# Weight operands made ahead and parked in DRAM, one unsplit intermediate, and last projections without GpSimd in a two-block kernel

## The chip, the cores and the metric

The kernel runs on one core of a Trainium2 chip. The metric is device time in microseconds for one launch. The time before is 2069.35 us, the median of three runs from 2067.27 to 2070.33. The profile shown is one execution by itself.

## The reference

Two blocks run one after the other on a sequence of 1024 tokens of width 1024, in fp32. The first has a mixer (three-pattern attention, a diagonal state-space branch, two gates) and a gated feed-forward part with a causal convolution. The second has three gated branches, whose projections are summed. Cut to what matters here:

```python
def _conv_ffn(u, w_up, w_conv, b_conv, w_down):        # block one
    a, val = jnp.split(u @ w_up, 2, axis=-1)           # 1024 -> 2 x 2048
    conv = b_conv
    for j in range(CONV_W):
        conv = conv + w_conv[j] * shifted(a, j)
    return (jax.nn.silu(conv) * val) @ w_down          # f, 2048 -> 1024

def _hybrid_layer(x, ...):                             # block two
    h = _rmsnorm_2(x, norm_g)
    p = h @ w_in                                       # 1024 -> 7680, twelve pieces
    ...
    y_a = (gmlp(u, v) * silu(z_a)) @ w_pa              # 512 -> 1024, three times
    y_b = (shortconv(x_b, b_g, c_g) * silu(z_b)) @ w_pb
    y_c = (pool(x_c) * silu(z_c)) @ w_pc
    merged = sigmoid(g_a) * y_a + sigmoid(g_b) * y_b + sigmoid(g_c) * y_c
    return x + merged @ w_o
```

## The kernel before

**Arithmetic.** Each fp32 operand of a product is split in two parts of type fp32r, high and low: ScalarE casts it (high), VectorE or GpSimd subtracts (low); `split` does both. Each product then takes three matmuls. A matmul here has 128 rows by 128 columns of weights and 512 moving columns.

**Strassen pairs.** The products with `w_up` (stage `ffn`) and with `w_in_2` (stages `gb` to `uz`) are made by seven products of half size rather than eight. The activations are combined into operands `s1` to `s4`, `a22` and others (class `X` in the code, four pieces k each, so that X.s2.3 is the piece 3 of s2); two blocks of weights make one pair, and are combined into b11, b21, t1 to t4 and b22 (class `Weights`). The weight sums are GpSimd operations (`pool` in `make`), the splits are ScalarE casts and VectorE subtractions. I write (0, t4) for the operand t4 of pair 0.

**Pairs begun early.** The activations come in two halves of tokens or rows, and the first half is ready sooner. For the first `NPF` = 4 pairs of `ffn` and the first `NPRE` = 6 of `gb` and `v2`, the products that need only the early half are made first, while `w_out` or the end of `down` (`lastdown`) still runs, with b11 and b21. Their other five operands, t2, t3, t1, t4 and b22, are made by the `late` entries of `make`, when the stage itself starts.

**Order.** The kernel first writes down all operations (class `Plan`); a list scheduler in it then orders them for all engines, by its own estimates, with limits on the buffers of each group (`nc.glim`). Each engine's queue runs in that order. That is why every instruction of the profile has line 458 (`issue`). `LEADR`, `LEADD`, `FLEAD` are the numbers of operations by which a load may be put ahead.

**Weights.** `Stream` walks a list of weight items (`_ITEMS`): `dma_to` loads ahead on SP's queue, `split_to` splits ahead, `get` gives a split item, `take` a raw one. `st.sa` says how many items ahead are split; it is 0 in the last stages.

**Stages**, by the trace, in us: v, us, gates and qk to 325; attn to 540; y1 to 605; w_out to 696; ffn to 1031; down to 1199; lastdown to 1258; gb to 1314; v2, B, C, gc, ga, uz to 1814; spat to 1834; yb to 1883; yc to 1926; ya to 1970; wo to the end.

**f.** `ffn` makes f in 16 tiles of 128 features by 1024 tokens, splits it and writes both parts to DRAM (`fs_d`), 32 writes on GpSimd's queue. `down` loads both parts again on SP's queue, half of the tokens at a time (`th` = 0, 1; 64 loads of 256 KB), multiplies each with the split weights `w_down` in steps `c` of two feature tiles, 48 matmuls for four row tiles, and, after the first half, transposes the rows for block two (`u3_tr`).

**Last projections.** `yb`, `yc` and `ya` run `gated`: for each item of weights the projection, times its gate, added to `mt`. The input of the next projection (`spilled`) is loaded and split; for `yc`, whose input is `cc_d`, the subtraction is GpSimd's, during `yb`. The additions to `mt` are GpSimd's in yb and yc.

Of the kernel before, what the change touches and what calls it, by code (L numbers as in the profile page):

```python
# [59 lines left out]
LEADR = 120  # L60
# [28 lines left out]
def _items():  # L89
# [384 lines left out]
def kernel(ctx: ExitStack, tc: tile.TileContext, x, wts, wada, vecs, rows, ssmv, wglu, ttab, iden,  # L474
# [11 lines left out]
    nc.glim = {"r": 5, "w": 14, "rr": NRR, "w2": NW2, "o": NO}  # L486
# [49 lines left out]
    fs_d = [dtile(f"f{i}_d", 16, F32R) for i in range(2)]  # L536
# [62 lines left out]
    class Stream:  # L599
# [159 lines left out]
    class Weights:  # L759


        def __init__(self, nk, order):
# [11 lines left out]
        def make(self, order):  # L774
            h = self.h

            def pool(o, a, b, op):
                nc.gpsimd.tensor_tensor(out=o, in0=a, in1=b, op=op)

            raws = {}  # L780
            for what, key in order:
# [3 lines left out]
                if what in ("pair", "early0", "late"):  # L785
# [8 lines left out]
                if what != "late":  # L794
                    self.operand((key, "b11"), b11)
                    yield
                    if what == "early0":
                        continue
# [21 lines left out]
        def pop(self, key):  # L820
# [1122 lines left out]
    for t in proj_half(me, 1, xsrc, hB, rowt):  # L1943
        if t % 4 == 0:
# [19 lines left out]
    W = Weights(4, early(NPF) + [("late", i) for i in range(NPF)] + [("pair", i) for i in range(NPF, 16)])  # L1964
# [12 lines left out]
    for i, n in enumerate(UPS):  # L1977
# [51 lines left out]
    for k in range(DAHEAD):  # L2029
        load_f(k, 0)  # L2030
    for th in range(2):
        full = [mm_ps(), mm_ps()]
        a, b = full
        pt = [[a[:, 0:512], a[:, 512:1024]], [b[:, 0:512], b[:, 512:1024]]] + [[tr_ps(), tr_ps()] for _ in range(2)]
        for c in range(7):
            w = [wA1(st.get()) for _ in range(2)]
# [19 lines left out]
        for i in range(2):  # L2056
            n = 16 * th + 14 + i + DAHEAD
            if n < 32:
                load_f(n % 16, n // 16)
# [393 lines left out]
```

## Time and profile before

| what | us |
|---|---|
| median of three runs | 2069.35 |
| the profiled execution, its own time | 2067.5 |
| its span in the trace | 2065.8 |
| TensorE busy | 1980.1 (96%) |
| VectorE busy | 1419.0 (69%) |
| ScalarE busy | 814.5 (39%) |
| GpSimd busy | 574.9 (28%) |

The mean granted TensorE clock is 0.982 of full speed. The trace gives each engine's instructions with start and length. An engine's idle time is put down to what released the instruction after it. The chain is followed back from the last instruction, always to what came last. Because TensorE is busy for nearly all of the span, a stretch is best read by counting its matmuls against its length.

### The profile page before, as it was taken

To read this page: it belongs to the slowest core of one execution; us is meant where nothing else is said; L and a number is where in the kernel's file an instruction comes from. 1 tells how busy PE (TensorE), PEld (TensorE's weight loads), DVE (VectorE), ACT (ScalarE), POOL (GpSimd) and SP (SyncE) were. 2 spreads that over 40 slices of the span, in tenths; PEclk is the share of its full clock that TensorE was granted. 3 is DMA by queue.
4 is the path that set the end of the run, shared out by engine and by line. 5 is a ranking of instruction groups with operands and counts; after the bars stand their busy time and mean duration, and the time that the engine had idled before them with its cause. 6 is when DMAs were issued, how large, how long until landed. Compare 5 with 4: busy or idle time off the path is not lost.

```text
span 2065.8 us, 24834 instructions
## 1 busy us (share of the span) xinstructions
PE 1980.1 (96%) x9174; PEld 1632.9 (79%) x9174; DVE 1419.0 (69%) x2246; ACT 814.5 (39%) x1277; POOL 574.9 (28%) x523
## 2 busy tenths in 40 slices
PE   5999999999999979999999998999999999989998
PEld 3788888888888757888888876887888888867887
DVE  8767765787664799777744469678878654673645
ACT  4413334667321634434432444343433433451212
POOL 4200202223201374333202038324323433121320
PEclk7999999999999999999999999999999999999999
DMA  8345444331833313423595513413212332264312
GB/s 338 113 156 194 165 146 107 102 100 57 319 129 142 118 51 131 145 92 119 194 355 174 209 71 134 152 45 109 86 70 95 128 112 105 71 244 143 112 52 82
DMA packets 88809, 282.23 MB, mean 137 GB/s; under 512 B 10224, under 2 KB 14672, under 8 KB 88688
## 3 DMA queue, kind: packets, MB, share of 16 engines
q1 hardware_dynamic: 58896, 186.72, 25.8%
q0 software_dynamic: 29792, 93.93, 13.3%
q8 instruction: 72, 1.18, 0.2%
q14 instruction: 49, 0.40, 0.1%
HBM read 206.62 MB, written 65.01 MB: 131 GB/s over the span
## 4 chain that ended last, share of the span: by engine, by line
PE 80%; issue 7%; DVE 6%; POOL 3%; DMA 2%; ACT 1%; SPq 0%; POOLq 0%; ACTq 0%; DVEq 0%
PE mm L458 41%; PE tr L458 39%; DVE s L458 6%; POOL s L458 3%; ACT s L458 1%; DMA s<-s 1%; DMA gs_d<-s 0%; DVE sm L458 0%; DMA s<-in_x_dram 0%; DMA vq_d<-s 0%; DMA g_d<-s 0%; DMA s<-in_wts_dram 0%; DMA v_d<-s 0%; SPq L458 0%; POOL gs_d L458 0%
## 5 line engine op out<-in xcount | busy, mean ns | idle before, releaser
L458 PE MATMUL mm<-s,s 128*128 128x512 f32 (+1 forms) x4424 | 1056.7, 394 | 28.8 <-DVE s L458 24.9
L458 PEld LDWEIGHTS mm<-s,s 128*128 128x128 f32 x4424 | 834.0, 190 | 209.8 <-DVE s L458 32.1
L458 PE MATMUL tr<-s,s 128*128 128x512 f32 (+3 forms) x4080 | 917.6, 378 | 25.1 <-DVE s L458 9.1
L458 PEld LDWEIGHTS tr<-s,s 128*128 128x128 f32 (+1 forms) x4080 | 719.6, 188 | 169.4 <-ACT s L458 15.6
L458 DVE TENSOR_TENSOR s<-s,s 128x512 fp32r<-128x512 f32 (+11 forms) x699 | 669.3, 986 | 149.2 <-ACT s L458 108.5
L458 ACT CAST s<-s 128x512 fp32r<-128x512 f32 (+4 forms) x556 | 382.7, 719 | 490.2 <-PE mm L458 161.0
L458 POOL TENSOR_TENSOR s<-s,s 128x512 f32<-128x512 f32 (+5 forms) x183 | 290.1, 1592 | 585.0 <-ACT s L458 317.4
L458 ACT ACTIVATE s<-s 128x1024 f32<-128x1024 f32 (+3 forms) x151 | 143.4, 952 | 318.5 <-DVE s L458 292.0
L458 DVE TENSOR_TENSOR s<-s,mm 128x512 f32<-128x512 f32 x184 | 125.5, 683 | 121.4 <-PE mm L458 120.8
L458 POOL TENSOR_TENSOR s<-s 128x512 f32<-128x512 f32 x92 | 141.9, 1545 | 118.1 <-DMA s<-in_wts_dram 58.9
L458 ACT COPY s<-tr 128x512 f32<-128x512 f32 (+2 forms) x160 | 85.0, 537 | 145.3 <-PE tr L458 143.0
L458 DVE SCALAR_TENSOR_TENSOR s<-s,s 128x1024 f32<-128x1024 f32 (+1 forms) x65 | 84.8, 1311 | 45.6 <-ACT s L458 44.3
L458 ACT ACTIVATE s<-s,sm 128x512 f32<-128x512 f32 (+7 forms) x119 | 90.6, 774 | 51.2 <-DVE sm L458 50.6
L458 DVE TENSOR_TENSOR s<-tr,s 128x512 fp32r<-128x512 f32 (+3 forms) x105 | 66.8, 652 | 61.6 <-PE tr L458 42.9
L458 PE MATMUL tr<-idn,s 128*128 128x128 f32 x608 | 92.8, 279 | 13.2 <-ACT s L458 8.5
L458 PEld LDWEIGHTS tr<-idn,s 128*128 128x128 f32 x608 | 74.0, 144 | 32.1 <-ACT s L458 11.9
L458 DVE SCALAR_TENSOR_TENSOR s<-s,mm 128x1024 f32<-128x1024 f32 x40 | 48.7, 1219 | 58.1 <-PE mm L458 58.1
L458 DVE TENSOR_TENSOR s<-s,tr 128x512 f32<-128x512 f32 (+1 forms) x90 | 52.6, 587 | 10.8 <-PE tr L458 5.2
L458 DVE SCALAR_TENSOR_TENSOR s<-s,vt,s 128x1023 f32<-128x1023 f32 (+1 forms) x40 | 54.7, 1368 | 4.4 <-ACT s L458 4.1
L458 POOL DMA_DIRECT2D f_d<-s x32 | 17.5, 548 | 114.1 <-ACT s L458 101.0
L458 ACT ACTIVATE s<-mm,hb 128x1024 f32<-128x1024 f32 x15 | 16.8, 1117 | 75.5 <-PE mm L458 67.0
L458 POOL DMA_DIRECT2D s<-s x48 | 25.2, 534 | 75.6 <-ACT s L458 60.8
(103 smaller groups left out, 654.6 us busy)
## 6 DMA issues: line engine op xcount, KB each, us to landing
s<-in_wts_dram SPq DMA_DIRECT2D x193, 512.0 KB, 4.3
s<-in_wada_dram SPq DMA_DIRECT2D x48, 512.0 KB, 5.9
f_d<-s POOLq DMA_DIRECT2D x32, 512.0 KB, 3.2
s<-f_d SPq DMA_DIRECT2D x64, 256.0 KB, 6.4
g_d<-s POOLq DMA_DIRECT2D x24, 512.0 KB, 3.1
s<-g_d SPq DMA_DIRECT2D x24, 512.0 KB, 8.4
s<-s POOLq DMA_DIRECT2D x32, 256.0 KB, 4.6
s<-in_x_dram SPq DMA_DIRECT2D x8, 512.0 KB, 9.0
```

The costliest lines, as they stand in the source:

```text
L458: hook(getattr(getattr(self.nc, eng), method)(*args, **kw), self.ops[i][7] + f"|{self.start[i]:.0f}|{i}")
```

## The change

It has five parts.

1. **Late operands.** A new generator, `store`, makes the five late operands of a pair ahead of their stage: it loads the pair's two raw blocks (SP's queue), makes the four sums on VectorE, splits (ScalarE and VectorE) and writes each operand, 512 KB, to DRAM (`wd_d`, GpSimd's queue). The 4 pairs of `ffn` are stored during `y1` and `w_out`, one step for each tile; the 6 of `gb` and `v2` during `down`, three or four steps for each `c`. Where `make` had `late` entries, it has `stored` ones: five loads on SP's queue, up to `LEADS` = 150 operations ahead. The raw blocks for this are appended to the items.
2. **f unsplit.** `ffn` writes f as it is, 16 writes. `down` loads it and splits it there (`load_f`, `split_f`).
3. **down's second half** makes the first three steps for row tiles 0 and 1, then `u3_tr`, and only then those steps for row tiles 2 and 3.
4. **Last projections.** The split of `cc_d` and the additions to `mt` go from GpSimd to VectorE, and from `spat` on `st.sa` is 2.
5. `LEADR` goes from 120 to 140.

Operations in the program: VectorE from 2182 to 2250, ScalarE from 1155 to 1171, GpSimd from 519 to 501, SP from 409 to 427, TensorE 9062 in both.

```diff
+SA2 = 2
+LATE = ("t2", "t3", "t1", "t4", "b22")
+LEADS = 150
-LEADR = 120
+LEADR = 140
...
+            def fetch(key, name):
+                t = slot("wb", F32R, group="w2")
+                load(f32(t), f32(wd_d[self.base + key][name]), nc.sync, LEADS)
+                self.w[key, name] = t[:, 0:h], t[:, 512:512 + h]
...
+                if what == "stored":
+                    for name in LATE:
+                        fetch(key, name)
+                        yield
...
+    def store(keys):
+        for key in keys:
+            r = [slot("r", group="ps") for _ in range(2)]
+            for i in range(2):
+                load(r[i], wts[_NITEM + 2 * key + i], nc.sync, LEADS)
+            (b11, b21), (b12, b22) = ((t[:, 0:512], t[:, 512:1024]) for t in r)
+            def put(name, src):
+                t = slot("ws", F32R, group="ps")
+                split(t[:, 0:512], t[:, 512:1024], src)
+                nc.gpsimd.dma_start(out=wd_d[key][name], in_=t)
+            tt(b12, b22, b12, ALU.subtract)
+            tt(b11, b12, b11, ALU.add)
+            yield
+            put("t2", b11)
...
-        hi, lo = slot("fh", F32R), slot("fl", F32R)
-        split(hi, lo, pv)
-        nc.gpsimd.dma_start(out=fs_d[0][n], in_=hi)
-        nc.gpsimd.dma_start(out=fs_d[1][n], in_=lo)
+        nc.gpsimd.dma_start(out=f_d[n], in_=pv)
...
+    def split_f(m):
+        if m < 16:
+            r = fr.pop(m)
+            for i in range(2):
+                t = ft[2 * (m % 8) + i, m // 8] = slot("f", F32R)
+                split(t[:, 0:512], t[:, 512:1024], r[:, 512 * i:512 * i + 512])
...
+    st.sa = SA2
...
-            split(hi, lo, f, None, e)
+            split(hi, lo, f)
...
-                (tt if last else lambda o, x_, y_, op: nc.gpsimd.tensor_tensor(out=o, in0=x_, in1=y_, op=op))(
-                    g, g, mt[n + j], ALU.add)
+                tt(g, g, mt[n + j], ALU.add)
```

In the rows of the order, a name such as s_7004 is one tile in SBUF, tr_ and mm_ are PSUM; the number counts tiles in the order of the plan. VectorE at ffn's start, before: the first row is X.s2.0, `s_6959` and `s_6952` are the raw blocks of pair 0, `s_7009`, `s_7090` and `s_7147` the sums behind X.s2.1 to X.s2.3.

```order
L458 TENSOR_TENSOR s_7004<-s_6981,s_7004 128x512
L458 TENSOR_TENSOR s_7022<-s_6959,s_7022 128x512
L458 TENSOR_TENSOR s_7009<-s_7009,s_6748 128x512
L458 TENSOR_TENSOR s_7017<-s_6952,s_7017 128x512
L458 TENSOR_TENSOR s_7069<-s_7009,s_7069 128x512
L458 TENSOR_TENSOR s_7090<-s_6993 128x512
L458 TENSOR_TENSOR s_7063<-s_6959,s_7063 128x512
L458 TENSOR_TENSOR s_7097<-s_6952,s_7097 128x512
L458 TENSOR_TENSOR s_7090<-s_7090,s_6788 128x512
L458 TENSOR_TENSOR s_6986<-s_6952,s_6986 128x512
L458 TENSOR_TENSOR s_7128<-s_7090,s_7128 128x512
L458 TENSOR_TENSOR s_7147<-s_7011 128x512
```

The five rows that read `s_6959` or `s_6952` are (0, t2), (0, t3), (0, t4), (0, t1) and (0, b22); X.s2.3 comes five rows behind the last one shown. The same place of VectorE after, from X.s2.0 (`s_7172`) over X.s2.1 (`s_7229`) and X.s2.2 (`s_7261`) to X.s2.3 (`s_7270`):

```order
L473 TENSOR_TENSOR s_7172<-s_7137,s_7172 128x512
L473 TENSOR_TENSOR s_7178<-s_7178,s_6893 128x512
L473 TENSOR_TENSOR s_7216<-s_7157 128x512
L473 TENSOR_TENSOR s_7226<-s_7180 128x512
L473 TENSOR_TENSOR s_7229<-s_7178,s_7229 128x512
L473 TENSOR_TENSOR s_7216<-s_7216,s_6930 128x512
L473 TENSOR_TENSOR s_7226<-s_7226,s_6988 128x512
L473 TENSOR_TENSOR s_7261<-s_7216,s_7261 128x512
L473 TENSOR_TENSOR s_7270<-s_7226,s_7270 128x512
L473 TENSOR_TENSOR s_7246<-s_7157,s_7246 128x512
L473 TENSOR_TENSOR s_7276<-s_7180,s_7276 128x512
```

No weight operand stands between X.s2.0 and X.s2.3, and X.s3.2 and X.s3.3, the last two rows, now come behind X.s2.3. VectorE at the start of yb, before: two operands of yb's activations (`s_14872`, `s_14882`), then the low part of the second weight item (`s_14894`), then gates and the third item (`s_14956`).

```order
L458 SCALAR_TENSOR_TENSOR s_14614<-s_14614,mm_1167 128x1024
L458 SCALAR_TENSOR_TENSOR s_14872<-s_14448,s_14866 128x1024
L458 SCALAR_TENSOR_TENSOR s_14882<-s_14584,s_14874 128x1024
L458 TENSOR_TENSOR s_14894<-s_6572,s_14662 128x1024
L458 SCALAR_TENSOR_TENSOR s_14617<-s_14617,mm_1168 128x1024
L458 SCALAR_TENSOR_TENSOR s_14620<-s_14620,mm_1169 128x1024
L458 TENSOR_TENSOR s_14956<-s_11749,s_14746 128x1024
```

Here GpSimd has the first three splits of `cc_d` at the same time. The same place of VectorE after, where `s_15060` is the last operand of yb's activations:

```order
L473 SCALAR_TENSOR_TENSOR s_15022<-s_14600,s_15014 128x1024
L473 TENSOR_TENSOR s_15034<-s_11901,s_14890 128x1024
L473 TENSOR_TENSOR s_14736<-s_14736,tr_1198 128x512
L473 TENSOR_TENSOR s_14736<-s_14736,tr_1199 128x512
L473 SCALAR_TENSOR_TENSOR s_14769<-s_14769,mm_1202 128x1024
L473 SCALAR_TENSOR_TENSOR s_15060<-s_14736,s_15057 128x1024
L473 TENSOR_TENSOR s_15072<-s_12357,s_14897 128x1024
L473 TENSOR_TENSOR s_15095<-s_14789,s_15037 128x1024
L473 SCALAR_TENSOR_TENSOR s_14772<-s_14772,mm_1203 128x1024
L473 TENSOR_TENSOR s_15109<-s_14791,s_15062 128x1024
```

The second weight item was split some twenty rows ahead; `s_15034` and `s_15072` are the third and fourth, and the splits of `cc_d` (`s_15095`, `s_15109` and two more) follow in this queue. The third place is VectorE in down's first half, after: `s_9218` is a split of `w_down`, `s_9224` and `s_9231` of f.

```order
L473 TENSOR_TENSOR s_9273<-s_9228,s_9257 128x1024
L473 TENSOR_TENSOR s_9247<-s_9247 128x512
L473 SCALAR_TENSOR_TENSOR s_9277<-s_9277,s_9239 128x1024
L473 TENSOR_TENSOR s_9243<-s_9247,s_9243 128x512
L473 TENSOR_TENSOR s_9157<-s_9277,s_9157 128x1024
L473 TENSOR_TENSOR s_9312<-s_9243,s_9312 128x512
L473 TENSOR_TENSOR s_9295<-s_9247,s_9295 128x512
L473 TENSOR_TENSOR s_9333<-s_9283,s_9317 128x1024
L473 TENSOR_TENSOR s_9247<-s_9247,s_9243 128x512
L473 TENSOR_TENSOR s_9243<-s_9243 128x512
L473 TENSOR_TENSOR s_9286<-s_9247,s_9286 128x512
L473 TENSOR_TENSOR s_9300<-s_9270,s_9300 128x512
```

Before, this queue had only splits of `w_down` here (with ffn's last operations). Now the sums (`s_9247`, `s_9243`) and splits (`s_9312`, `s_9295`, `s_9286`) of the first stored pair stand between the splits of `w_down` (`s_9273`, `s_9333`) and of f (`s_9300`).

## Rows read from the trace of the kernel before

**Rows 1.** The page: busy time of the engines; share of the chain.
```profile
PE 1980.1 (96%) x9174; PEld 1632.9 (79%) x9174; DVE 1419.0 (69%) x2246; ACT 814.5 (39%) x1277; POOL 574.9 (28%) x523
...
PE 80%; issue 7%; DVE 6%; POOL 3%; DMA 2%; ACT 1%; SPq 0%; POOLq 0%; ACTq 0%; DVEq 0%
```
**Rows 2.** Stretches: length, PE, PEld, DVE, ACT, POOL (instructions), clock, DMA share, GB/s.
```profile
527.00:605.00 78.00, 78.00 (x352) 64.91 (x353) 47.88 (x45) 21.27 (x24) 10.49 (x20) 1.00 0.67 247
605.00:697.00 92.00, 91.47 (x420) 75.47 (x418) 51.93 (x76) 24.58 (x48) 10.66 (x17) 1.00 0.42 150
697.00:820.00 123.00, 107.94 (x450) 84.24 (x449) 115.85 (x130) 58.41 (x95) 69.97 (x47) 0.94 0.28 98
860.00:1031.00 171.00, 170.38 (x751) 140.61 (x750) 131.94 (x149) 71.51 (x101) 55.78 (x49) 1.00 0.39 133
1031.00:1060.00 29.00, 29.00 (x129) 24.02 (x128) 15.39 (x14) 8.97 (x9) 3.70 (x7) 1.00 1.05 407
1060.00:1199.00 139.00, 139.00 (x629) 114.61 (x629) 60.29 (x69) 46.65 (x58) 12.53 (x11) 1.00 0.56 198
1199.00:1249.00 50.00, 46.64 (x215) 38.16 (x214) 40.39 (x48) 27.56 (x48) 29.51 (x19) 0.97 0.17 64
1249.00:1315.00 66.00, 59.91 (x254) 46.84 (x253) 54.68 (x59) 28.88 (x45) 45.72 (x36) 1.00 0.52 180
1814.00:1834.00 20.00, 20.00 (x106) 16.70 (x105) 18.48 (x21) 16.98 (x22) 0.00 (x0) 1.00 1.03 410
1834.00:1883.00 49.00, 38.30 (x147) 29.70 (x146) 20.83 (x15) 6.80 (x8) 11.19 (x4) 0.86 0.27 92
```
**Rows 3.** The chain, 1828 to 1850: start, us, what.
```profile
1831.36 0.44 PE tr L458 x4
```
**Rows 4.** Groups by form, TensorE, 697 to 820: short transposes.
```profile
L458 PE MATMUL tr<-idn,s 128*128 128x128 f32 x32 | 4.5, 282 | 0.4 <-ACT s L458 0.4
```
**Rows 5.** Groups by form: VectorE 1031 to 1199; ScalarE, GpSimd 860 to 1031.
```profile
L458 DVE TENSOR_TENSOR s<-s,s 128x512 fp32r<-128x512 f32 x9 | 5.8, 685 | 2.7 <-ACT s L458 2.7
...
L458 ACT CAST s<-s 128x512 fp32r<-128x512 f32 x54 | 30.3, 619 | 3.6 <-PE tr L458 2.5 <-POOL s L458 1.1
...
L458 POOL DMA_DIRECT2D f_d<-s x18 | 9.9, 550 | 79.9 <-ACT s L458 73.4 <-DVE s L458 6.5
```
**Rows 6.** Timeline of VectorE, 714 to 741: start, us, operation, count.
```profile
724.56 8.51 DVE L458 TENSOR_TENSOR s<-s,s 128x512 fp32r<-128x512 f32 x5
```
**Rows 7.** The chain, 725 to 756: start, us, what.
```profile
726.27 12.46 DVE s L458 x8
...
738.80 4.45 DMA s<-in_wts_dram
...
743.39 10.23 POOL s L458 x6
```
**Rows 8.** DMA issues, KB, us to landing: whole span; 1031 to 1060; 527 to 575.
```profile
s<-in_wts_dram SPq DMA_DIRECT2D x193, 512.0 KB, 4.3
...
s<-in_wts_dram SPq DMA_DIRECT2D x6, 512.0 KB, 10.9
...
s<-ga_d POOLq DMA_DIRECT2D x8, 512.0 KB, 15.9
```
**Rows 9.** Timeline of TensorE, 1214 to 1224, with idle time before.
```profile
1218.67 5.51 PE L458 MATMUL tr<-s,s 128*128 128x512 f32 x16 [3.36 <-ACT s L458]
```
**Rows 10.** Timelines of TensorE, VectorE and GpSimd around yb's start.
```profile
1844.73 12.75 PE L458 MATMUL mm<-s,s 128*128 128x512 f32 x44 [7.62 <-DVE s L458]
...
1829.88 1.23 DVE L458 SCALAR_TENSOR_TENSOR s<-s,s 128x1024 fp32r<-128x1024 f32 x1 [0.29 <-ACT s L458]
...
1835.77 5.63 DVE L458 SCALAR_TENSOR_TENSOR s<-s,s 128x1024 fp32r<-128x1024 f32 x2
1841.43 3.24 DVE L458 TENSOR_TENSOR s<-s,s 128x1024 fp32r<-128x1024 f32 x1
...
1834.64 8.96 POOL L458 TENSOR_TENSOR s<-s,s 128x1024 fp32r<-128x1024 f32 x3 [38.50 <-ACT s L458]
```

More of the change, by code (lines that the diff above doesn't have):

```diff
@@ L53 @@
 LEADO = 100
-DAHEAD = 4
+FA = 2
+NB2 = 3
 LEADD = 150
@@ L143, in _items @@
             it.append(("WP", None, 0, 0, 0))
-        raw("w_in_2", n, o[a])
-        raw("w_in_2", m, o[b])
+        if i >= NPRE:
+            raw("w_in_2", n, o[a])
+            raw("w_in_2", m, o[b])
     it.append(("WS", None, 0, 0, 0))
@@ L152, in _items @@
             it.append(("A", "w_o_2", k, 512 * h, 512))
-    return it
-_ITEMS = _items()
+    k = len(it)
+    for n in UPS[:NPF]:
+        it.append(("B", "w_up", n, 0, 128))
+        it.append(("B", "w_up", n, 2048, 128))
+    for n, a, m, b in ps[:NPRE]:
+        it.append(("B", "w_in_2", n, o[a], 128))
+        it.append(("B", "w_in_2", m, o[b], 128))
+    return it, k
+_ITEMS, _NITEM = _items()
 def _item_cols(i):
@@ L535 @@
     o1_d = dtile("o1_d", max(NPF, NPRE))
-    fs_d = [dtile(f"f{i}_d", 16, F32R) for i in range(2)]
+    wd_d = [{n: dram.tile([128, 1024], F32R, name=f"wd{i}_{n}") for n in LATE} for i in range(NPF + NPRE)]
+    f_d = dtile("f_d", 16)
     bb_d = dtile("bb_d", 4)
@@ L784, in make @@
                     continue
-                if what in ("pair", "early0", "late"):
+                if what == "stored":
+                    for name in LATE:
+                        fetch(key, name)
+                        yield
+                    continue
+                if what in ("pair", "early0"):
                     r1 = raws[key] = st.take()
@@ L793, in make @@
                     continue
[L794 to L798, printed above, removed]
+                self.operand((key, "b11"), b11)
+                yield
+                if what == "early0":
+                    continue
                 r2 = st.take()
@@ L804, in make @@
                 yield
-                if what == "pair":
-                    self.operand((key, "b21"), b21)
-                    yield
+                self.operand((key, "b21"), b21)
+                yield
                 self.operand((key, "t3"), b12)
@@ L1845 @@
     me = Act()
+    stored = store(range(NPF))
     for n in range(8):
+        for _ in range(STY):
+            next(stored, None)
         load_g(n + 1)
@@ L1905 @@
     for t in proj_half(me, 0, xsrc, hA, rowt):
+        for _ in range(STO):
+            next(stored, None)
         nc.gpsimd.dma_start(out=h_d[t][:, 0:512], in_=hA(t))
@@ L1943 @@
     for t in proj_half(me, 1, xsrc, hB, rowt):
+        for _ in range(STO if t < 7 else 99):
+            next(stored, None)
         if t % 4 == 0:
@@ L1963 @@
     st.sa = 0
-    W = Weights(4, early(NPF) + [("late", i) for i in range(NPF)] + [("pair", i) for i in range(NPF, 16)])
+    W = Weights(4, early(NPF) + [("stored", i) for i in range(NPF)] + [("pair", i) for i in range(NPF, 16)], 0)
     def second_half():
@@ L2028 @@
     st.dma_to(st.i + 3)
-    for k in range(DAHEAD):
-        load_f(k, 0)
+    for m in range(FA):
+        load_f(m)
+    for m in range(FA - 1):
+        split_f(m)
+    stored = store(range(NPF, NPF + NPRE))
     for th in range(2):
@@ L2055 @@
             load_h(4 * th + n)
[L2056 to L2059, printed above, removed]
+        load_f(8 * th + 7 + FA)
+        split_f(8 * th + 7 + FA - 1)
         for j in range(4):
@@ L2103 @@
     st.sa = 0
-    W = Weights(4, early(NPRE) + [("late", i) for i in range(NPRE)]
-                + [("pair", i) for i in range(NPRE, 14)] + [("item", "wp")] + [("pair", i) for i in range(14, NP)])
+    W = Weights(4, early(NPRE) + [("stored", i) for i in range(NPRE)]
+                + [("pair", i) for i in range(NPRE, 14)] + [("item", "wp")] + [("pair", i) for i in range(14, NP)], NPF)
     def second_half():
```

86 lines of the change are left out of this document (59 added, 27 removed).

## The prediction

> **What bounds the kernel now.** I read the busy line and the chain first [rows 1]. TensorE is busy for 1980.1 of 2065.8 us and its own work makes up 80% of the chain that ends last, so time is to be had only where TensorE waits, or runs slowly after a wait. Next I read one row for each stretch [rows 2]. In the undisturbed one, 860 to 1031, 751 matmuls fill 171.00 us at a granted clock of 1.00: 0.2277 us each. That is the ruler. A stretch's length minus its count times 0.2277 is what it loses, whether in gaps or at a low clock; the 128-column transposes are shorter, four in 0.44 us [rows 3], so each takes 0.117 off the expected time.
>
> - ffn's start, 697 to 820: 450 x 0.2277 = 102.5, less 32 x 0.117 = 3.7 for short transposes [rows 4], is 98.7 of 123. **24.3 us lost.**
> - last projection of block one, 1199 to 1249: TensorE busy 46.64 of 50. **At least 3.4 lost**, by idle time alone.
> - start of w_in_2, 1249 to 1315: 254 x 0.2277 = 57.8 of 66. **8.2 lost.**
> - yb, 1834 to 1883: 147 x 0.2277 = 33.5 of 49. **15.5 lost.**
> - y1, w_out and down, 527 to 697 and 1031 to 1199: TensorE busy 169.5 of 170 and 168 of 168. **Nothing lost**, and this is where the change puts new work.
>
> Why ffn's start loses: VectorE is busy 115.85 of 123 us there and GpSimd 69.97, against 131.94 of 171 and 55.78 later [rows 2]. The same 128x512 subtraction takes VectorE 0.68 us with GpSimd nearly idle [rows 5] and 1.7 here: five in 8.51 us [rows 6]. The chain of waits through the worst part has nothing of TensorE in it [rows 7]: VectorE to 738.7, then a weight load of 4.45 us that could start only then, then six GpSimd sums, 10.23 us, up to 753.6, then a cast and two VectorE operations.
>
> **The change part by part.** The sum starts from the profiled execution: span 2065.8, measured 2067.5. The median of the three runs is 2069.35, 1.85 above, and I add that at the end.
>
> *Late operands at ffn's start.* Before X.s2.3, the operand on which the first full product waits, VectorE's queue held the five late operands of the first pair at 1.77 each (8.9 us) and three operations moved behind it now (X.s3.2 and X.s3.3 at 1.76, X.s1.0 at 0.68: 4.2 us). X.s2.3 ended at 741.0; without 13.1 us of that it ends near 728. The product of (0, t4) began near 753, once VectorE had emptied an accumulator, and that stood in its queue behind splits for the second pair; the load of [rows 7] and two of its six sums are that pair's too. All of these go, so I count 13 to 15 us for this product as well: 738 to 740. Loads replace the making: 20 of 512 KB, in place of 4 raw ones, in a stretch whose DMA share is 0.28 [rows 2], at 4.3 us each [rows 8], and issued up to 150 instructions ahead, while TensorE still runs w_out: hidden. Behind the first product the gain holds, since 15 more late operands and 12 GpSimd sums are gone up to 820: by the mean of VectorE's 130 operations there (0.89) 13 of its 115.85 us, and each that stays gets nearer to 0.68. What stays lost is the wait for VectorE's activation sums themselves from 715 on, some 6 to 7 us. **Gain 17**; bounds 10 (only the 8.9 + 1 us of the first pair) and 22 (all but 2).
>
> *Start of w_in_2.* The same with six pairs. VectorE is busy 54.68 of 66 us and GpSimd 45.72 [rows 2]. Thirty late operands and their 24 sums go from here and the stretches behind; VectorE's 59 operations here take 0.93 us each, and 27 of them make late operands: 25 us, which leaves it under half filled. **Gain 7.5 of 8.2**; bounds 5 and 8.
>
> *Last projection, block one.* The 3.4 us are one wait for a ScalarE copy that stands behind activation work [rows 9]; that order stays, and only GpSimd's weight sums beside it go. **Gain 1** (0 to 3).
>
> *yb.* At 1834.64 GpSimd starts three 128x1024 splits of the next input, 8.96 us, and beside them VectorE takes 5.63 us for two operations that take 1.22 to 1.24 each elsewhere, and 3.24 for the split of the second weight item [rows 10]; then TensorE goes on at 1844.73 after 7.62 us. The clock row for the stretch is 0.86 [rows 2], so part of the 15.5 is paid after the gap. The change takes each of the three causes away: the splits go to VectorE (4 x 1.22, behind), so nothing slows it, and the weight items are split two ahead, the second one before yb starts. It costs one split of 1.22 in 1814 to 1834, where VectorE is busy 18.48 of 20 [rows 2]. VectorE then has some 32 us of work for 31 us of TensorE around yb's end, so it is nearly the bound itself; I leave 1 us. **Gain 14.5**; bounds 11 and 16. What hides the sums of yb and yc on VectorE (7 x 1.22 = 8.5 us, from GpSimd's 2.4 to 3.2 each) is VectorE's idle half in 1883 to 1926.
>
> *What making ahead costs in y1 and w_out.* Four pairs: 20 splits and 16 sums, 36 x 0.68 = 24.5 us on VectorE, which is busy 47.88 + 51.93 of 170 [rows 2]: 124 of 170. On the queues 8 loads and 20 writes, 14.7 MB, beside 19.3 + 13.8 MB (247 GB/s x 78, 150 x 92): 281 GB/s on average. The highest rate shown is 410 [rows 2], and y1's first 45 us run there already: loads then took 15.9 us [rows 8]. No wait on TensorE appears in these stretches, so the slack isn't visible; bounds 0 and 4, **cost 1**.
>
> *The same in down.* Six pairs: 30 splits and 24 sums, 54 x 0.68 = 36.7; and f's splits move here from ffn: 32 x 0.68 = 21.8. VectorE goes from 15.39 + 60.29 [rows 2] to 134 of 168 us. DMA: 12 loads and 30 writes, 22 MB, less 8.4 MB because f is read once at half the size: 39.3 + 13.6 = 53 MB, 315 GB/s average, with the first 29 us already at 407 and its weight loads at 10.9 us rather than 4.3 [rows 2, 8]. ScalarE takes 62 casts more, 62 x 0.62 = 38 us [rows 5] on 55.6 of 168 [rows 2]. All three have room on average; in the first 60 us the queues don't. Bounds 0 and 10, **cost 3**.
>
> *In ffn* 16 casts, 16 subtractions of 1024 and 16 of 32 DMA issues on GpSimd go (0.55 each [rows 5]): no gap between 860 and 1031, so nothing gained.
>
> By row, GpSimd's issue of a DMA stays at 0.55 us beside a VectorE busy 77% of the time [rows 2, 5]. The Trainium skill, page "SBUF — State Buffer", section "SBUF: two separate sides", speaks against more writes from GpSimd: VectorE can lock GpSimd out of the shared port so that it can't write descriptors, and a DMA of about 620 ns took about 3100. By that rule the 30 writes of down would hold GpSimd some 75 us longer, which fits in its 168 us but would delay h_d's loads behind them; by the row it costs nothing, and I go by the row.
>
> Sum: 17 + 7.5 + 1 + 14.5 - 1 - 3 = 36. 2067.5 - 36 = 2031.5, plus 1.85: **2033**. By the bounds alone: -26 + 14 = 12 less, and -49 + 0 = 49 less.
>
> **The rivals.**
>
> *A. ffn's start stays bound.* GpSimd still makes the activation operands (about 14 operations at 1.7) beside VectorE, so every VectorE operation up to 735 keeps its 1.77; if in addition fetched operands land at 10 to 16 us as in the crowded stretches [rows 8], TensorE waits on those instead. Then only the first pair's 8 us are gained: 2042. For it: the contention is in the rows. Against: fetches can start a hundred instructions early, in a stretch at 0.42 of the DMA's time. 0.12. That the change doesn't do what it says at ffn would read the same way.
>
> *B. New waits in down or w_out.* VectorE's queue is filled to 80% and the queues to the ceiling for the first 60 us of down; f and w_down loads take turns with the writes. If TensorE waits for f or w_down there for 15 to 20 us more than my 3: 2050. 0.10.
>
> *C. Slower: the queue's head.* Engines take their instructions in order. A sum of store waits for its raw load; the w_down split and f's split that TensorE needs next stand right behind it. A load took up to 16 us in the saturated stretches [rows 8], and one step of down is 48 matmuls, 10.9 us, of cover. If each of the ten pairs stalled the queue for that cover and 4 us more, it would cost 40 us: 2073. From 36 us on the kernel is slower than before. Against: loads are issued up to 150 instructions before, and only the first sum of a pair waits for them; the splits after it don't. 0.05.
>
> **How the numbers follow.** Forecast 0.73, with its own range 2021 to 2041; A 0.12; B 0.10; C 0.05. The range reaches to A and B and leaves out C and the tails: **2020 to 2051**. A measurement of this kernel can tell some 0.2%, 4 us, from no change. Faster by more than that is the forecast, A and B, less 0.03 for a larger B that ends near no change: 0.92; same 0.03; slower 0.05.
>
> **What would show it.** In the trace after, ffn's start (up to its 450th matmul) should take 106 us rather than 123, X.s2.3 should end 12 to 14 us nearer to the stage's start, and no GpSimd sum of weights should stand there. w_in_2's start should have no gap over 1 us. yb should hold the clock at 1.00 with no gap of 7 us. Down should keep 168 us and VectorE rise to about 134; a gap on TensorE there whose releaser is VectorE behind a sum of store is C, one whose releaser is a load of f is B. Gaps at ffn's start released by DMA are A. The prediction is wrong if down or w_out grow by more than 10 us, or if VectorE's operations at 715 to 735 still decide when the first product of ffn ends.

## The result, and the profile after

The changed kernel takes 2032.63 us, the median of four runs from 2030.47 to 2035.2; before, measured again beside it, 2069.57. The ratio is 0.9824, with a 95% interval from 0.9807 to 0.9841. The prediction was 2033, with a range from 2020 to 2051. The profiled execution took 2033.6 us, with a span of 2031.9.

The busy line and the chain of the page, as in [rows 1]:

```profile
PE 1968.3 (97%) x9174; PEld 1631.6 (80%) x9174; DVE 1422.1 (70%) x2314; ACT 814.2 (40%) x1293; POOL 484.1 (24%) x505
...
PE 81%; issue 9%; DVE 5%; DMA 3%; POOL 1%; ACT 1%; SPq 0%; POOLq 0%; ACTq 0%; DVEq 0%
```

GpSimd lost 91 us of work. VectorE, which got 68 more operations, has only 3 us more: of its sums and subtractions of 128x512 in SBUF, 119 took over 1 us before and 73 do after; [rows 5, 6] show that length beside a busy GpSimd (1.7 us) and without it (0.68).

The stretches after, with the columns of [rows 2]: w_out, ffn's start, ffn's undisturbed part, down's first 29 us, the rest of down, lastdown, gb, and spat with yb.

```profile
605.00:700.00 95.00, 92.51 (x415) 76.21 (x414) 64.11 (x96) 31.63 (x61) 16.51 (x29) 0.98 0.67 234
700.00:823.00 123.00, 117.44 (x528) 94.92 (x527) 99.08 (x124) 52.34 (x82) 43.37 (x34) 1.00 0.46 160
850.00:1017.00 167.00, 167.00 (x739) 138.27 (x738) 122.14 (x143) 65.15 (x101) 46.69 (x39) 1.00 0.31 109
1017.00:1046.00 29.00, 29.00 (x130) 24.01 (x128) 24.92 (x33) 16.69 (x25) 7.99 (x15) 1.00 1.02 384
1046.00:1186.00 140.00, 139.56 (x631) 115.12 (x630) 95.25 (x126) 65.01 (x95) 24.59 (x32) 1.00 0.81 288
1186.00:1239.00 53.00, 47.98 (x221) 39.26 (x220) 44.61 (x55) 29.36 (x51) 26.77 (x17) 0.97 0.25 89
1239.00:1294.00 55.00, 55.00 (x244) 45.54 (x243) 17.32 (x25) 11.20 (x15) 11.24 (x14) 1.00 0.95 351
1797.00:1849.00 52.00, 52.00 (x247) 43.25 (x246) 38.58 (x38) 22.39 (x27) 0.00 (x0) 1.00 0.65 240
```

In the first 123 us of ffn TensorE now issues 528 matmuls, where it issued 450 (the prediction gave 106 us to 450 of them; the 450th behind 700 starts at 806). gb and yb have no idle time left. Down is as full of TensorE work as before, with VectorE busy for 120 us in it rather than 76. lastdown still has 5 us of idle time, and w_out has some where it had half a microsecond.

For a comparison of all kernels below I took, for each TensorE instruction of a trace, the time until the next one starts beyond what it takes at full clock, and summed that by stage of the program (us):

| kernel | gates | w_out | ffn | down | lastdown | gb | B | gc | spat, yb | all |
|---|---|---|---|---|---|---|---|---|---|---|
| before | 7.0 | 1.9 | 27.3 | 1.9 | 6.6 | 8.7 | 6.2 | 0.5 | 17.2 | 138.5 |
| after | 8.5 | 5.3 | 9.7 | 2.3 | 8.1 | 0.2 | 7.2 | 3.2 | 0.8 | 105.1 |
| yb_undo | 7.1 | 3.7 | 9.8 | 2.3 | 7.9 | 0.2 | 4.5 | 3.4 | 14.7 | 114.9 |
| yb_ahead | 8.4 | 5.2 | 9.7 | 2.3 | 8.1 | 0.8 | 6.2 | 3.4 | 0.8 | 104.7 |
| yb_vector | 4.9 | 3.8 | 9.9 | 2.3 | 8.3 | 0.4 | 4.4 | 3.4 | 15.5 | 113.6 |
| before_ahead | 6.5 | 1.9 | 27.4 | 1.9 | 6.6 | 8.8 | 4.8 | 0.5 | 0.8 | 122.1 |
| ffn_late | 6.7 | 1.9 | 20.9 | 2.3 | 3.6 | 0.2 | 1.8 | 3.4 | 0.8 | 103.1 |
| ffn_pool | 8.8 | 5.1 | 13.9 | 2.3 | 3.7 | 0.2 | 4.8 | 3.4 | 0.8 | 104.9 |
| gb_late | 8.5 | 5.3 | 9.8 | 2.0 | 6.0 | 12.0 | 2.6 | 3.3 | 0.8 | 112.3 |
| f_split | 8.4 | 4.0 | 23.3 | 22.9 | 10.5 | 0.2 | 1.7 | 2.6 | 0.8 | 135.3 |
| u3_first | 8.4 | 3.8 | 9.8 | 16.1 | 6.6 | 0.4 | 3.3 | 3.1 | 0.8 | 113.3 |
| down_twice | 5.1 | 3.8 | 9.8 | 9.8 | 13.8 | 0.2 | 1.8 | 3.4 | 0.8 | 109.6 |
| ld_vector | 5.2 | 3.9 | 9.8 | 2.3 | 1.6 | 2.7 | 3.8 | 3.3 | 0.8 | 94.4 |
| both_vector | 8.2 | 3.9 | 9.3 | 2.3 | 0.3 | 1.8 | 3.7 | 2.3 | 0.8 | 93.1 |

gates and B are not what any of these kernels is about; over the kernels of the table they differ by up to 4 and 5.5 us. There is one trace of each kernel, so whether the execution or the scheduler's order makes that difference is not shown. A difference of a few microseconds in "all" therefore says nothing; one of 5 us within the stage that was edited is the least that I read.

Before to after: ffn -17.6, spat and yb -16.4, gb -8.5; w_out +3.4, gc +2.7, lastdown +1.5, gates +1.5, B +1.0, down +0.4.

### The profile page after: what moved, and what is told of

Its sections match the earlier page's. It is cut to its first block, busy times and chain, and to the rows that moved or that the text cites. A ratio compares the mean times of both kernels' runs of the same rounds, so it can differ in the third digit from the quotient of the medians.

```text
span 2031.9 us, 25039 instructions
## 1 busy us (share of the span) xinstructions
PE 1968.3 (97%) x9174; PEld 1631.6 (80%) x9174; DVE 1422.1 (70%) x2314; ACT 814.2 (40%) x1293; POOL 484.1 (24%) x505
## 4 chain that ended last, share of the span: by engine, by line
PE 81%; issue 9%; DVE 5%; DMA 3%; POOL 1%; ACT 1%; SPq 0%; POOLq 0%; ACTq 0%; DVEq 0%
PE mm L473 42%; PE tr L473 39%; DVE s L473 5%; ACT s L473 1%; DMA s<-s 1%; POOL s L473 0%; DMA gs_d<-s 0%; DVE sm L473 0%; DMA wd_t<-s 0%; DMA s<-in_x_dram 0%; DMA g_d<-s 0%; DMA vq_d<-s 0%; DMA v_d<-s 0%; POOL h_d L473 0%; SPq L473 0%
## 5 line engine op out<-in xcount | busy, mean ns | idle before, releaser
L473 PE MATMUL mm<-s,s 128*128 128x512 f32 (+1 forms) x4424 | 1046.4, 392 | 11.2 <-DVE s L473 9.4
L473 DVE TENSOR_TENSOR s<-s,s 128x512 fp32r<-128x512 f32 (+10 forms) x747 | 657.9, 913 | 128.7 <-ACT s L473 89.7
L473 POOL TENSOR_TENSOR s<-s,s 128x512 f32<-128x512 f32 (+4 forms) x151 | 220.9, 1470 | 410.6 <-ACT s L473 230.4
L473 POOL TENSOR_TENSOR s<-s 128x512 f32<-128x512 f32 x72 | 101.4, 1410 | 139.8 <-DVE s L473 86.2
L473 DVE TENSOR_TENSOR s<-s,tr 128x512 f32<-128x512 f32 (+1 forms) x90 | 52.7, 588 | 31.7 <-DMA g_d<-s 11.8
L473 DVE SCALAR_TENSOR_TENSOR s<-s,vt,s 128x1023 f32<-128x1023 f32 (+1 forms) x40 | 56.2, 1406 | 12.0 <-ACT s L473 11.8
L473 ACT ACTIVATE s<-s,vt 128x1024 f32<-128x1024 f32 x20 | 24.9, 1245 | 74.4 <-DVE s L473 48.9
L473 POOL DMA_DIRECT2D wd_t<-s x40 | 21.4, 534 | 101.7 <-DVE s L473 90.8
```

The lines of the kernel that those rows point to most:

```text
L473: hook(getattr(getattr(self.nc, eng), method)(*args, **kw), self.ops[i][7] + f"|{self.start[i]:.0f}|{i}")
```

## The experiments

All are the kernel after with one edit, but for before_ahead. They ran in three groups; the kernel before, run beside each, took 2067.8, 2070.13 and 2069.94. Part 5, `LEADR` at 140, was undone in none of them.

**yb_undo, yb_ahead, yb_vector: what in part 4 was it?** The first undoes the part; the second keeps only the weights split ahead; the third keeps only the work taken from GpSimd.

```diff
# yb_undo: both; yb_ahead: the second and third alone; yb_vector: the first alone
-    st.sa = SA2
+    st.sa = 0
...
-            split(hi, lo, f)
+            split(hi, lo, f, None, e)      # e = nc.gpsimd for cc_d
...
-                tt(g, g, mt[n + j], ALU.add)
+                (tt if last else lambda o, x_, y_, op: nc.gpsimd.tensor_tensor(...))(g, g, mt[n + j], ALU.add)
```

> The kernel after, with the last projections as before: splits of cc_d and sums of yb and yc on GpSimd, weights not split ahead. If part 4 of the change has its whole gain in yb, spat to yb loses 15 to 17 us as in the kernel before, with a gap of 7 to 8 us, and the time is 2047 to 2050. If the gain there came from elsewhere (earlier loads, another order), yb keeps most of it: under 2040.

> The kernel after with the GpSimd work of the last projections back, but weights still split two items ahead. Theory contention (VectorE's operations are stretched by GpSimd's splits beside them): two operations of yb's activations still take 5.6 us rather than 2.5, a gap of about 4 us and a spell of half clock stay, so 2037 to 2043. Theory order (the second weight item's split was last in the queue, and that alone was the wait): under 2 us lost in yb, so 2032 to 2035.

> The kernel after with no GpSimd in the last projections, and weights not split ahead. Theory contention: VectorE's operations take 1.23 us each, the second item's split ends some 5 us earlier than before, the gap shrinks to 2 to 3 us: 2034 to 2038. Theory order: the split of the second item still stands behind two operations, and VectorE now has the splits of cc_d too: a gap of 4 us or more, 2038 to 2045.

Measured: yb_undo 2043.85, under the 2047 to 2050 that I had expected; yb_ahead 2034.39, as theory order had it; yb_vector 2048.39 (2041.95 to 2048.95), above both theories. Undoing the part brings 13.9 us of loss back in its place. Splitting ahead is all of the gain: yb_ahead can't be told from the kernel after. Taking the work from GpSimd is worth nothing alone. The trace of yb_vector is of its fastest execution; where the other three lose 6 us more isn't shown. In yb_vector nothing runs beside VectorE. Its timeline, first VectorE, then TensorE (idle time before it in brackets):

```profile
1812.07 2.35 DVE L473 SCALAR_TENSOR_TENSOR s<-s,s 128x1024 fp32r<-128x1024 f32 x2
...
1829.86 5.11 DVE L473 TENSOR_TENSOR s<-s,s 128x1024 fp32r<-128x1024 f32 x4
...
1815.62 12.84 PE L473 MATMUL mm<-s,s 128*128 128x512 f32 x44 [2.21 <-DVE s L473]
...
1835.03 1.22 PE L473 MATMUL mm<-s,s 128*128 128x512 f32 x2 [3.77 <-DVE s L473]
```

And the stretch in the columns of [rows 2]:

```profile
1810.00:1857.00 47.00, 38.06 (x146) 29.49 (x145) 19.98 (x18) 6.70 (x7) 0.00 (x0) 0.85 0.28 93
```

The two operations that took 5.63 us in [rows 10] take 2.35, and the wait of 7.62 us falls to 2.21. But the splits of cc_d now stand in VectorE's queue ahead of the next weight item's, and there a new wait of 3.77 us appears. With the half clock that follows these waits (0.85 over the stretch, 0.86 in [rows 2]) the loss is nearly the same, 15.5 us against 17.2. In yb_ahead GpSimd still makes those splits; VectorE, GpSimd and TensorE in its timeline:

```profile
1812.51 2.35 DVE L473 SCALAR_TENSOR_TENSOR s<-s,s 128x1024 fp32r<-128x1024 f32 x2
...
1820.84 2.41 POOL L473 TENSOR_TENSOR s<-s,s 128x1024 fp32r<-128x1024 f32 x1 [42.54 <-PE tr L473]
...
1820.45 9.81 PE L473 MATMUL mm<-s,s 128*128 128x512 f32 x42
```

The weight split done early also changes the order, so that GpSimd starts 8 us behind the two operations, and they aren't stretched. The edit thus removes both the queue place and the overlap; these runs don't separate the two any further.

**before_ahead: the same line alone, in the kernel before.**

```diff
+    st.sa = 2
     def spilled(src, e=None):
```

> The kernel before, with one change alone: weights split two items ahead in the last projections; GpSimd keeps the splits of cc_d and the sums. If the place of the second item's split in VectorE's queue was all of yb's loss, as yb_ahead says: yb loses under 1.5 us rather than 17, 2051 to 2056. If the rest of the change matters to it: above 2058.

Measured: 2053.27, ratio to before 0.9932 (0.9909 to 0.9954). One line gives 16 of the change's 37 us, and nothing else of the change is needed for it.

**ffn_late, gb_late: one stage's pairs made late again.**

```diff
# ffn_late
-    stored = store(range(NPF))
-    W = Weights(4, early(NPF) + [("stored", i) for i in range(NPF)] + ...
+    W = Weights(4, early(NPF) + [("late", i) for i in range(NPF)] + ...
# gb_late: the same for store(range(NPF, NPF + NPRE)) and the second W
```

> The kernel after, with the late operands of ffn's four pairs made at ffn's start again (nothing stored in y1 and w_out). My theory: ffn's start loses its 17 to 18 us again, w_out gets back 2 to 3: 2045 to 2050. Rival (ffn's gain came from f unsplit and the fewer GpSimd issues, or from the order): ffn keeps more than half of its gain: under 2040.

> The kernel after, with the late operands of the six pairs of w_in_2 made at gb's start again (nothing stored in down). My theory: gb loses its 8 to 9 us again, down and lastdown give back 0 to 2: 2039 to 2042. Rival B in small (the stored pairs cost in down and lastdown what they save in gb): within 3 us of 2032.6.

Measured: ffn_late 2031.46 (2029.14 to 2031.86), where I had expected 2045 to 2050; gb_late 2037.65, where I had expected 2039 to 2042. ffn_late's time is the rival's, but not for its reason: ffn kept 6.4 us of its gain of 17.6, less than half. The stretches of ffn_late (w_out, ffn's start) and gb's start in gb_late:

```profile
605.00:697.00 92.00, 91.68 (x421) 75.70 (x419) 51.94 (x75) 24.05 (x46) 10.01 (x16) 1.00 0.42 148
697.00:823.00 126.00, 114.76 (x484) 91.45 (x485) 116.75 (x134) 59.44 (x97) 65.43 (x46) 0.95 0.25 90
...
1240.00:1306.00 66.00, 59.52 (x241) 47.58 (x240) 49.19 (x56) 28.00 (x44) 42.77 (x35) 0.92 0.46 160
```

By stage, storing ffn's four pairs saves 11.2 us in ffn (20.9 to 9.7) and costs 3.4 in w_out. The rest of what it saves is not seen in the time, because lastdown lost 4.5 us less in ffn_late, where the scheduler put a ScalarE copy elsewhere (behind the sixth square rather than the eighth, and TensorE waits 1.12 us for it rather than 5.02; see ld_vector), and B 5.4 less, which varies anyway. So ffn's pairs are worth some 8 us in place, and nothing that I could measure in sum. Of ffn's 17.6 us, 6.4 came without them. With f in two parts the same pairs are worth less: from before to f_split, below, ffn's loss falls only from 27.3 to 23.3. For gb the term stands: 11.8 us lost again there, 2.1 given back in lastdown, 4.6 in B, 5 us in the time.

**ffn_pool: were it VectorE's splits or GpSimd's sums?**

```diff
                     for name in LATE:
                         fetch(key, name)
+                        if self.base == 0 and name != "b22":
+                            z, (q, p) = slot("zz"), self.w[key, name]
+                            pool(z[:, 0:512], f32(q), f32(p), ALU.add)
```

> The kernel after, with a GpSimd sum of 128x512 beside each of the first four fetched operands of ffn's four pairs (16 sums, as many as the making took); their results are not used. Theory count (VectorE's five splits per pair were the cost at ffn's start): ffn stays within 3 us: 2032 to 2036. Theory contention (GpSimd's 16 sums slowed VectorE's own operations, and delayed GpSimd's activation operands): ffn's start loses 8 us or more: 2041 to 2047.

Measured: 2033.54. GpSimd in its first 60 us of ffn has the sums, the twelve of this row among them:

```profile
L473 POOL TENSOR_TENSOR s<-s 128x512 f32<-128x512 f32 x12 | 16.8, 1414 | 9.0 <-DMA s<-wd_t 3.8 <-DVE sm L473 2.0 <-ACT s L473 1.9
```

The time is theory count's. ffn loses 13.9 rather than 9.7: GpSimd's sums bring back 4 of the 11 us. That would leave 7 to VectorE's own splits and the loads, if these sums, which wait for the fetched operands (9.0 us of the row), cost what the old ones did; that isn't shown. Again lastdown (3.7 rather than 8.1) hides it in the sum.

**f_split, u3_first: parts 2 and 3 undone.**

```diff
# f_split
-        nc.gpsimd.dma_start(out=f_d[n], in_=pv)
+        hi, lo = slot("fh", F32R), slot("fl", F32R)
+        split(hi, lo, pv)
+        nc.gpsimd.dma_start(out=fs_d[0][n], in_=hi)
+        nc.gpsimd.dma_start(out=fs_d[1][n], in_=lo)
# and down loads both parts, splits nothing
# u3_first
-NB2 = 3
+NB2 = 0
```

> The kernel after, with f split in ffn and kept in two parts in DRAM as before (32 writes of 512 KB in ffn, 64 loads of 256 KB in down). With the late operands made at ffn's start (ffn_late) ffn still lost 20.9 us by the stage table against 27.3 before, so 6 us of its gain are not theirs. Theory f (ffn's 16 casts, 16 subtractions and 16 of 32 DMA issues were in the way until the first pairs' backlog was gone): ffn loses 3 to 6 us more than the 9.7 of after, down loses the same or less: 2034 to 2039. Theory order (those 6 us are the scheduler's other order and the later start): ffn within 1.5 us of after, 2030 to 2034.

> The kernel after, with the transposes for block two's first rows ahead of all of the second half's products in down, as before, rather than behind three steps of two row tiles. Theory: down had no gap there before and has 1 us or so of them now, so within 3 us of 2032.6. Rival: with VectorE's queue now filled in down, the transposes' evictions come late, and a gap of 5 us or more appears around the middle of down: 2037 to 2042.

Measured: f_split 2064.04 (2059.83 to 2068.71), u3_first 2041.79. For f_split both theories missed, by 25 us and more; for u3_first the rival's range held. TensorE's waits over all of f_split's down (us in total, times, longest):

```profile
PE mm L473 <- ACT s L473: 16.6, 2, 10.2
```

The DMA issues from 1043 to 1190 (KB each, median us to landing), loads of w_down and the raw blocks first:

```profile
s<-in_wts_dram SPq DMA_DIRECT2D x30, 512.0 KB, 12.9
...
wd_t<-s POOLq DMA_DIRECT2D x17, 512.0 KB, 11.3
```

And ScalarE's timeline, with the cast behind which the longest wait ends:

```profile
1187.96 1.04 ACT L473 CAST s<-s 128x1024 fp32r<-128x1024 f32 x1 [10.96 <-DMA s<-in_wts_dram]
```

This is rival B: a load of w_down lands late, ScalarE's cast waits 11 us for it and TensorE 10.2. (Before the shorter wait, 6.4 us at 1042, ScalarE waited for VectorE and not for a load.) Why it was late stands in SP's own timeline, and in the two stretches around its pause:

```profile
1144.91 10.66 SPq L473 DMA_DIRECT2D s<-f_d  x4
1166.08 0.81 SPq L473 DMA_DIRECT2D s<-in_wts_dram  x2
1166.98 4.91 SPq L473 DMA_DIRECT2D s<-f_d  x8
1173.29 12.50 SPq L473 DMA_DIRECT2D s<-in_wts_dram  x8
```

```profile
1155.00:1166.00 11.00, 11.00 (x63) 9.10 (x62) 5.82 (x6) 5.45 (x7) 0.00 (x0) 1.00 0.16 49
1166.00:1188.00 22.00, 12.88 (x59) 10.33 (x57) 7.79 (x11) 3.81 (x6) 3.75 (x7) 0.89 0.97 346
```

For 10 us SP issued nothing, with the DMA engines at 0.16; its longest wait there, 10.8 us, was for TensorE. Then ten loads went out at once, eight of them parts of f, and the load in question, issued behind them at 1173.29, landed at 1187.86. So the queues were not full all along. They ran empty and were then filled in one burst, and the load that TensorE needed stood behind it. For which buffer SP had waited, and whether it was f's, isn't shown. With f unsplit, in the kernel after, 30 such loads from 1046 to 1186 land in 6.3 us:

```profile
s<-in_wts_dram SPq DMA_DIRECT2D x30, 512.0 KB, 6.3
```

GpSimd has as many writes `wd_t` in both stretches, 17; it is SP's own queue that has more, 40 loads of f rather than 16, of 256 KB each. ffn lost 23.3 us in f_split, so f unsplit was worth 13.6 there too: 7.2 more than the 6.4 that came without the stored pairs (before to ffn_late, which has `LEADR` and the scheduler's other order in it too). In u3_first TensorE waits for the evictions of the transposes, around down's middle; its eight longer waits on transposes from 1110 to 1150, and the stretch:

```profile
PE tr L473 <- DVE s L473: 3.4, 4, 0.8
PE tr L473 <- ACT s L473: 3.2, 4, 1.1
```

```profile
1110.00:1150.00 40.00, 31.71 (x128) 23.51 (x127) 32.28 (x55) 24.84 (x38) 8.17 (x12) 0.83 0.62 211
```

Before, the same order had no such wait; VectorE was busy for 75.7 us of down there, and for 120 in the kernel after. Part 3 is worth 13.8 us in down and 9 in the time, but only with the fuller queue; the stores and f's splits, which both fill it, weren't tried apart.

**down_twice: how near is down to its edge?**

```diff
                 nc.gpsimd.dma_start(out=wd_d[key][name], in_=t)
+                if key >= NPF:
+                    nc.gpsimd.dma_start(out=we_d[key - NPF][name], in_=t)
```

> The kernel after, with each operand that down stores written twice, the second time to a place that nobody reads: 30 more writes of 512 KB on GpSimd's queue, 15.7 MB. Theory slack (down's queues have room on average, and loads are issued far ahead): down grows by under 3 us: 2032 to 2036. Theory ceiling (the loads of f and w_down take turns with the writes, and down is at its edge): gaps on TensorE released by VectorE or ScalarE behind a load or a buffer, 10 to 25 us: 2043 to 2058.

Measured: 2041.08, between the two theories. Down's part behind 1043 as a stretch, its DMA issues, and TensorE's waits from 1014 to 1222:

```profile
1043.00:1190.00 147.00, 142.46 (x629) 115.16 (x628) 89.29 (x119) 63.75 (x94) 38.69 (x60) 0.99 0.93 343
```

```profile
s<-in_wts_dram SPq DMA_DIRECT2D x32, 512.0 KB, 10.2
wd_t<-s POOLq DMA_DIRECT2D x19, 512.0 KB, 14.7
```

```profile
PE tr L473 <- ACT s L473: 8.3, 1, 8.3
PE mm L473 <- DVE s L473: 3.3, 3, 1.6
PE mm L473 <- ACT s L473: 2.8, 2, 2.3
```

30 more writes cost 7.5 us in down. lastdown loses 5.7 more too, in the wait of 8.3 us at 1216, where ScalarE's copy again stands behind squares that wait for GpSimd's products; as that wait changes with the scheduler's order (ffn_late), it can't be put down to the writes. With 288 GB/s in down's part behind its start (after) there is hardly a loss, 2.3 us, with 343 there is. The Trainium skill, page "DMA: Bandwidth & Descriptors", section "Queues, rings and completion order", says that a DMA engine takes turns between the queues that have work for it. This run agrees: SP has 32 such loads here and 30 in the kernel after, and they land in 10.2 rather than 6.3 us beside GpSimd's doubled writes.

**ld_vector, both_vector: GpSimd's remaining elementwise work.** The wait in lastdown of the kernel after: TensorE, then ScalarE.

```profile
1207.05 5.29 PE L473 MATMUL tr<-s,s 128*128 128x512 f32 x15 [5.02 <-ACT s L473]
...
1203.69 1.06 ACT L473 ACTIVATE s<-s 128x1024 f32<-128x1024 f32 x1 [1.07 <-POOL s L473]
...
1205.37 1.06 ACT L473 ACTIVATE s<-s 128x1024 f32<-128x1024 f32 x1 [0.54 <-DVE s L473]
...
1206.43 0.56 ACT L473 COPY s<-tr 128x512 f32<-128x512 f32 x1
```

The copy that empties a PSUM bank stands behind two squares that wait for GpSimd's and VectorE's products.

```diff
# ld_vector
-            (nc.vector if t in (3, 7) else nc.gpsimd).tensor_tensor(out=a, in0=a, in1=gfr, op=ALU.mult)
+            (nc.vector if t > 3 or t == 3 else nc.gpsimd).tensor_tensor(out=a, in0=a, in1=gfr, op=ALU.mult)
# both_vector: that, and in Seven.rest
-            v, g = nc.vector, nc.gpsimd
+            v, g = nc.vector, nc.vector
```

> The kernel after with all four products of the second half's rows with g_final (lastdown) on VectorE, three of them on GpSimd before. The wait of 5.2 us for a ScalarE copy at the end of lastdown: theory contention (GpSimd's products of 2.4 to 3.4 us and VectorE's operations stretched to 3.25 and 2.85 beside them make the squares late, and the copy stands behind these): the gap shrinks to 1 to 3 us, 2027 to 2031. Theory queue (the copy stands behind four squares on ScalarE whatever they wait for): the gap stays at 4 us or more, 2031 to 2035.

> ld_vector (lastdown's products on VectorE, 2027.3) with the 14 GpSimd operations of the activations' late combinations on VectorE too, at the starts of ffn and of w_in_2. Theory contention (rival A's half: VectorE's operations up to X.s2.3 take 1.77 beside GpSimd's): VectorE's operations there take 0.68, X.s2.3 ends 3 to 6 us earlier, ffn loses 4 to 7 rather than 9.8: 2021 to 2026. Theory count (VectorE then has 14 more to do, 0.68 each, 9.5 us): no gain or a loss, 2027 to 2033.

Measured: ld_vector 2027.31 (ratio to before 0.9802, 0.9788 to 0.9817), both_vector 2022.45 (0.9781, 0.9758 to 0.9804). In ld_vector TensorE runs through the place:

```profile
1197.71 11.50 PE L473 MATMUL tr<-s,s 128*128 128x512 f32 x50
```

lastdown loses 1.6 rather than 8.1 us, and gb 2.7 rather than 0.2. The time is theory contention's. But the copy also moved: it stands behind the fifth square here, behind the eighth in the kernel after, and in ffn_late, with the products still on GpSimd, its other place alone took 4.5 us off. How much is GpSimd's and how much the copy's place, these runs don't tell apart. both_vector's operations up to X.s2.3 take 0.68 us each, as expected, but ffn's loss stays at 9.3: what is saved there is given back at once, when VectorE's evictions come late behind the added operations:

```profile
728.87 8.52 DVE L473 TENSOR_TENSOR s<-s,s 128x512 fp32r<-128x512 f32 x14 [0.23 <-ACT s L473]
738.82 3.10 DVE L473 TENSOR_TENSOR s<-s,s 128x512 fp32r<-128x512 f32 x5 [1.42 <-ACT s L473]
...
742.57 2.08 PE L473 MATMUL tr<-s,s 128*128 128x512 f32 x4 [3.08 <-DVE s L473]
```

So theory count holds at ffn, though the time lies in theory contention's range. Both kernels are faster than the kernel after; whether both_vector beats ld_vector is not settled, since the intervals overlap and the stages differ by 1 or 2 us.

## Why the prediction was right, and where it wasn't

The time was right, to 0.4 us. That it came so near is in part luck: the four runs lie 5 us apart, and terms that were off by up to 2.7 us either way cancel. The profiled execution gained 33.9 us where the sum said 36. By terms:

- **ffn's start**: 17 foreseen, 17.6 measured. X.s2.3 ends 13.5 us after X.s2.0 starts, where it was 25.9: 12.4 nearer, 13.1 counted. By the clock of the trace it ends at 735.7 rather than the 728 foreseen, because X.s2.0 itself starts 7 us later than before, at 722.2. In the kernel after, GpSimd and VectorE at this place:

```profile
725.00 10.16 POOL L473 TENSOR_TENSOR s<-s,s 128x512 f32<-128x512 f32 x6 [0.63 <-DVE s L473]
...
727.16 14.58 DVE L473 TENSOR_TENSOR s<-s,s 128x512 fp32r<-128x512 f32 x15
...
744.12 16.16 PE L473 MATMUL mm<-s,s 128*128 128x512 f32 x70 [1.27 <-DVE s L473]
```

  From X.s2.0 to the product of (0, t4) it is 22 us, where [rows 6, 7] belong to a way of 38. Rival A's half is still there: beside GpSimd, VectorE's operations up to X.s2.3 mostly take 1.77 us as before, but TensorE's longest wait behind them is 1.27. But the step that gave all of it to the late operands failed: they are worth 11.2 there with f unsplit (ffn_late), and 4.0 without (f_split). The two parts earn the 17.6 together. I had put f's casts at nothing, because TensorE has no gap between 860 and 1031. The first tiles of f, though, fall into the backlog up to 830: before, the writes of four of the sixteen are issued by 815.
- **gb**: 7.5 foreseen, 8.5 measured, and gb_late shows the cause.
- **yb**: 14.5 foreseen, 16.4 measured. The size was right, the reason half wrong: I named three causes and had the change remove each. Splitting ahead alone does it (yb_ahead, before_ahead); taking GpSimd's work away alone does nothing (yb_vector).
- **lastdown**: a gain of 1 foreseen, a loss of 1.5 measured. I took the order as fixed; the scheduler put one more square ahead of the copy, the eighth. Before, two of the squares ahead of it wait for GpSimd's products too (1.05 and 1.01 us); the prediction named activation work there, but only GpSimd's weight sums as what could go.
- **y1 and w_out**: a cost of 1 foreseen, 1.8 to 3.4 measured, over the kernels that store there. It is rival C's mechanism in small. TensorE, then ScalarE, at 657:

```profile
657.46 3.05 PE L473 MATMUL tr<-s,s 128*128 128x512 f32 x7 [2.49 <-DVE s L473]
...
655.42 0.63 ACT L473 ACTIVATE s<-s 128x512 f32<-128x512 f32 x1 [4.75 <-DMA wd_t<-s]
```

  A square's scratch buffer had just held a stored operand, and ScalarE waited 4.75 us for its write to land. The wait was for a buffer behind a write, not for a load, which no rival of mine had named.
- **down**: a cost of 3 foreseen, 0.4 measured, VectorE at 120 us rather than 134. That down stayed free is the work of parts 2 and 3. I counted the bytes that f unsplit saves, but gave neither part a price; without the one down loses 20.6 us more, without the other 13.8. Rival B was thus nearer than 0.10 suggests: without part 2 it comes true (f_split). Without part 3 the wait is another, for the evictions of transposes.
- **Not foreseen**: gc +2.7. All kernels made from the kernel after have 2.3 to 3.4 there, those from the kernel before 0.5. Its cause wasn't tried.
- **GpSimd's issues**: by the profile's page 40 of the writes took 0.53 us each to issue, beside a VectorE busy for most of the time, as [rows 5] had it. The rule of the Trainium skill, page "SBUF — State Buffer", section "SBUF: two separate sides", that VectorE, while it runs a copy that takes both ports, keeps GpSimd from writing descriptors, is not seen in these issues, beside a VectorE that mostly adds, subtracts and multiplies:

```profile
L473 POOL DMA_DIRECT2D wd_t<-s x40 | 21.4, 534 | 101.7 <-DVE s L473 90.8
```

So the right sum hides terms that were credited wrongly. At ffn and in down they don't show in it because the misjudged credit stayed within the change: what I gave to one part, another had earned.

## What to carry to other kernels

Before a heavy change to a queue, look for the one instruction that TensorE waits for and ask whether it could simply stand earlier: one line gave 16 of 37 us here. Work moved into a stretch without gaps is free only as long as its queues have room, so price the bytes and the queue places that the same change gives back there, and look at the transfer rate in short stretches; parts that look like tidying may be what pays for the rest. And when a scheduler makes the order, compare edits stage by stage: two edits whose sums were equal differed by 11 us in the stage that they were about.

## What was not expected of the hardware

Write-backs hold their SBUF buffers longer than I had thought. A 512 KB write of a stored operand lands in 7.9 us in the median of the kernel after, and in down in 11.3 in f_split and 14.7 in down_twice, against 2.9 for f's writes in the kernel after. Loads on SP's queue slow as well, from 6.3 to 10.2 us beside twice the writes, and to 12.9 in f_split. The mean rate of a stage doesn't show that coming: in f_split it was 49 GB/s for 11 us and 346 for the next 22, with the DMA engines busy for 0.97 of these.

```profile
wd_t<-s POOLq DMA_DIRECT2D x40, 512.0 KB, 7.9
...
f_d<-s POOLq DMA_DIRECT2D x16, 512.0 KB, 2.9
```
